# Sums of squares, first gate weights and output weights moved: three stages of an encoder-block kernel on one core

## The chip, the cores and the metric

The kernel runs on one core of one Trainium2 chip. The metric is the device time of one execution in microseconds (us), taken as the median of several runs.

The core's engines run side by side, each with its own queue of instructions: PE (TensorE) multiplies matrices into PSUM banks, PEld is its weight load, DVE (VectorE), ACT (ScalarE) and POOL (GpSimd) work element by element, and SP (SyncE) issues the loads and stores. An instruction that waits holds everything behind it on its own engine.

## The reference, cut to what matters

One encoder block on x of 1024 tokens by 1024 channels, all in float32:

```python
h = rmsnorm(x, norm_gain)
q, k, v, gate_a, u_in, v_in, gate_b, g_merge = split(h @ w_in)
q, k = rope(rmsnorm(q, q_gain)), rope(rmsnorm(k, k_gain))  # 8 q heads, 2 kv heads of 64
attn = block_attention(q, k, v) * silu(gate_a)
y_a = attn @ w_proj_attn
vv = layernorm(gelu(v_in))
v_mix = einsum('gij,bcjgd->bcigd', w_spatial, vv) + b_spatial
y_b = (gelu(u_in) * v_mix * silu(gate_b)) @ w_proj_gmlp
g = sigmoid(g_merge + b_merge)                             # two gates of 1024 channels
y = g[0] * y_a + g[1] * y_b
out = rmsnorm(x + y @ w_out, final_gain)
```

## The kernel before, in words

**Precision.** Each float32 operand is split into a rounded high part and a low part, the rest (`split`, line 115). The high part is a cast on the engine handed in (`hi_part`, line 107: lines 109 on POOL, 111 on ACT), the low part a subtraction, mostly on DVE (line 117). A product is then three matmuls: high by high, high by low, low by high (`mm3`, lines 175 to 177). So each block of weights or x costs one cast and one subtraction before PE can use it.

**Order.** The code is written stage after stage, and a scheduler then reorders the instructions of each engine within their dependences. Which buffer a tile gets is set by its tag and the number of buffers of that tag: a tile waits until the last reader of the buffer's former holder is done. PSUM has a tag "S" with three double banks, and single banks "o" and "z".

**Start.** `load_x` (line 146) brings the eight 128x1024 blocks of x transposed, multiplies them by the gain and splits them (line 159 on ACT, 160 on DVE). Each block goes straight into the k and v product (`kv`). High parts of the kv weights and the v weights are cast on POOL (`stream_w`, `nat_weights`, with `NWE` as the engines). Beside that, `add_square` squares every block on ACT (line 171, tiles of tag "og"); POOL and DVE add the squares up (line 172, `XSQ` names the engine of each block), and 16 small matmuls sum over the partitions (line 236, `ssx`). From them comes `rstd`, one over the root mean square of each token, and its half `rstdh`. `nat_group` makes the groups v0 to v3 in "S" banks; ACT moves each out with `rstdh` as the scale (line 371, `vst`). Then come GELU and layer norm of v (`v_post`), mixing over the 128 tokens of a chunk (`spatial`), the q groups, the norm of q and k (`head_norm`, line 319 for its last product) and the rotary positions (`rope`): their cross products stand on POOL (line 330, four of 128x256 for each q group and four for k). The tables behind them (line 395) and two scalings of v (lines 407 and 428) are POOL's too.

**Attention.** For each of 32 pairs PE makes two score tiles, softmax runs over DVE and ACT (lines 557 to 568), a DMA transposes the probabilities, and PE mixes them with v into the bank "o" (line 579, evacuated by lines 580 to 586). The products u, gate a and gate b fill PE between.

**Projections and gates.** `proj_b` makes the spatial branch's projection in eight blocks `yb0` to `yb7` (ACT copies each out, line 641), while `x_chunk` builds sums and differences of x (`xf`) for the gates. The gates and the other projection are done in pairs by `seven` products instead of eight. For each gate pair i, `pair_weights` (step "w" in the list `MORDER`) loads two rows of 512 KB (`graw`), squares their four quarters on ACT into the bank "o" (line 817, `gsq`), of which only the sums are kept, and makes a common scale from the sums (`unit_scale`, lines 673 to 680: a small matmul, DVE, POOL, DVE). `pair` (step "g") splits the scaled weights into two 16-bit parts (line 684 on ACT, 685 on DVE: `wg`) and multiplies. `p1g` is the copy of a pair's first product, to which the others are added (line 700). Step "A" makes the forms of the attention output (`gf`, `gk`), steps "a" project them (`wp`, `y`). Step "o" loads the output weights.

**Output weights and output product.** `out_weights` loads 16 halves of 256 KB through the four small `wraw` tiles, casts each (ACT, line 111, `woh`) and subtracts (DVE, line 117, `wol`). `split_y` splits the merged y blocks (lines 864 and 865). 384 matmuls make the output, and `finish` adds x (`xr`, line 950), takes the norm and stores.

## Time and profile before

| | before |
|---|---|
| runs | 766.96, 770.64, 770.91 us |
| median | 770.64 us |
| profiled execution | 771.03 us, of which the span is 769.3 us |
| PE busy | 94% of the span |
| VectorE, ScalarE, GpSimd busy | 80%, 57%, 21% |
| granted clock of TensorE, mean | 0.979 |

The span runs from the first to the last instruction on the chip; the time has some 1.7 us more around it. A row of the timeline gives start, length, engine, line, operation, the tiles it writes and reads, and in brackets how long its engine was idle before it and what ended that. A row of the grouped lines gives the count, busy time, the mean of one in ns and the idle time before them. In a row of windows each engine has its busy us and its number of instructions.

### The profile page before, as it was taken

To read this page: it belongs to the slowest core of one execution; us is meant where nothing else is said; L and a number is where in the kernel's file an instruction comes from. 1 tells how busy PE (TensorE), PEld (TensorE's weight loads), DVE (VectorE), ACT (ScalarE), POOL (GpSimd) and SP (SyncE) were. 2 spreads that over 40 slices of the span, in tenths; PEclk is the share of its full clock that TensorE was granted. 3 is DMA by queue.
4 is the path that set the end of the run, shared out by engine and by line. 5 is a ranking of instruction groups with operands and counts; after the bars stand their busy time and mean duration, and the time that the engine had idled before them with its cause. 6 is when DMAs were issued, how large, how long until landed. Compare 5 with 4: busy or idle time off the path is not lost.

```text
span 769.3 us, 9864 instructions
## 1 busy us (share of the span) xinstructions
PE 725.2 (94%) x3577; PEld 535.9 (70%) x3577; DVE 612.9 (80%) x915; ACT 434.7 (57%) x752; POOL 160.1 (21%) x131
## 2 busy tenths in 40 slices
PE   7989999998999899999999997899999998799996
PEld 7868888776888677788777884355464645388884
DVE  6965897699888989988889999999888898833223
ACT  7304457386878877878777478555474535521101
POOL 4930665345123221123200000010000000000000
PEclk9979999998999999999999999999999999999998
DMA  7321120135668779869899930130030204520211
GB/s 279 106 82 35 29 82 16 40 58 109 135 137 149 145 146 163 176 133 172 165 192 267 250 84 1 55 120 19 20 117 1 71 27 152 170 102 29 82 55 55
DMA packets 152609, 81.27 MB, mean 106 GB/s; under 512 B 135408, under 2 KB 136048, under 8 KB 152560
## 3 DMA queue, kind: packets, MB, share of 16 engines
q1 hardware_dynamic: 152272, 80.36, 42.5%
q8 instruction: 28, 0.46, 0.2%
q10 hardware_dynamic: 288, 0.28, 0.1%
q14 instruction: 21, 0.17, 0.1%
HBM read 42.88 MB, written 4.19 MB: 61 GB/s over the span
## 4 chain that ended last, share of the span: by engine, by line
PE 53%; DVE 21%; DMA 11%; ACT 6%; issue 6%; POOL 2%; SPq 1%; POOLq 0%; DVEq 0%; ACTq 0%
DMA T<-p 8%; PE out L175 4%; PE out L177 4%; PE out L176 4%; PE o L579 3%; DVE p L568 3%; DVE nm L557 2%; PE g L175 2%; PE g L176 2%; PE g L177 2%; DMA wraw<-in_wall_dram 2%; PE v L176 1%; PE v L177 1%; PE s L554 1%; PE v L175 1%
## 5 line engine op out<-in xcount | busy, mean ns | idle before, releaser
L568 DVE SCALAR_TENSOR_TENSOR p<-P,ri,p 128x1024 f16<-128x1024 f32 x64 | 85.8, 1343 | 22.2 <-ACT p L567 21.8
L567 ACT ACTIVATE p<-P,ri 128x1024 f16<-128x1024 f32 x64 | 73.1, 1143 | 25.1 <-DMA T<-p 17.4
L561 ACT ACTIVATE P<-s,nm 128x1024 f32<-128x1024 f32 x64 | 71.3, 1114 | 24.1 <-DVE nm L557 15.6
L557 DVE TENSOR_REDUCE nm<-s 128x1 f32<-128x1024 f32 x64 | 77.7, 1215 | 1.8 <-PE s L555 1.4
L579 PE MATMUL o<-T,vS 128*128 128x256 f16 x512 | 63.5, 278 | 4.9 <-ACT qT L355 2.9
L579 PEld LDWEIGHTS <-vS 128*128 128x128 f16 x512 | 48.2, 99 | 19.8 <-issue 8.0
L117 POOL TENSOR_TENSOR wl<-wraw,wh 128x512 fp32r<-128x512 f32 x24 | 38.8, 1620 | 101.3 <-ACT wh L111 57.4
L554 PE MATMUL s<-kT,qT 128*128 128x512 f32 x128 | 53.5, 418 | 4.0 <-ACT P L561 4.0
L677 POOL TENSOR_TENSOR scg<-scg,mhalf 128x1 f32<-128x1 f32 x8 | 7.0, 870 | 217.2 <-DVE scg L676 217.2
L555 PE MATMUL s<-kT,qT 128*128 128x512 f32 x128 | 50.5, 395 | 0.0
L950 DVE TENSOR_TENSOR xr<-out,xr 128x1024 f32<-128x1024 f32 x7 | 8.6, 1224 | 46.4 <-PE out L177 46.2
L898 ACT ACTIVATE sq<-xr 128x1024 f32<-128x1024 f32 x7 | 7.4, 1060 | 64.1 <-DVE xr L950 64.1
L175 PE MATMUL out<-woh,yhl 128*128 128x512 f32 x96 | 38.0, 396 | 0.0
L177 PE MATMUL out<-woh,yhl 128*128 128x512 f32 x96 | 37.6, 392 | 0.0
L176 PE MATMUL out<-wol,yhl 128*128 128x512 f32 x96 | 37.6, 391 | 0.0
L554 PEld LDWEIGHTS s<-kT,qT 128*128 128x128 f32 x128 | 24.1, 188 | 11.0 <-ACT P L561 6.4
L900 POOL TENSOR_TENSOR rs<-rs,mhalf 128x1 f32<-128x1 f32 x7 | 3.8, 549 | 125.5 <-DVE rs L899 125.5
L555 PEld LDWEIGHTS s<-kT,qT 128*128 128x128 f32 x128 | 24.1, 189 | 4.6 <-issue 0.2
L492 PE MATMUL ga<-xh,wh 128*128 128x512 f32 x64 | 26.1, 408 | 1.2 <-DVE ga30w L498 1.1
L175 PE MATMUL v<-nh,xh 128*128 128x512 f32 x64 | 26.8, 419 | 0.0
L492 PE MATMUL u<-xh,wh 128*128 128x512 f32 x64 | 25.6, 400 | 0.8 <-DVE uw L515 0.8
L177 PE MATMUL v<-nh,xl 128*128 128x512 f32 x64 | 26.1, 408 | 0.0
(554 smaller groups left out, 2212.9 us busy)
## 6 DMA issues: line engine op xcount, KB each, us to landing
wraw<-in_wall_dram SPq DMA_DIRECT2D x75, 256.0 KB, 3.1
graw<-in_wall_dram SPq DMA_DIRECT2D x16, 512.0 KB, 5.1
xraw<-in_xT_dram SPq DMA_DIRECT2D x15, 512.0 KB, 6.8
xr<-in_x_dram SPq DMA_DIRECT2D x8, 512.0 KB, 4.3
out_dram<-xr SPq DMA_DIRECT2D x7, 512.0 KB, 2.6
T<-p SPq DMA_TRANSPOSE x64, 4.5
wspr<-in_wsp_dram SPq DMA_DIRECT2D x2, 256.0 KB, 2.6
rtk<-in_cst_dram SPq DMA_DIRECT2D x1, 512.0 KB, 4.4
```

What stands on the lines that cost most here:

```text
L117: eng_lo.tensor_tensor(out=lo, in0=raw, in1=hi if hi.dtype == F16 else hi.bitcast(F32), op=ALU.subtract)
L175: pe.matmul(o, ah, bh, start=start, stop=False)
L176: pe.matmul(o, ah, bl, start=False, stop=False)
L177: pe.matmul(o, al, bh, start=False, stop=stop)
L492: pe.matmul(o, wh[:, C(dt % 4)], xh[dt][:, H(h)], start=(dt == 0), stop=False)
L554: pe.matmul(sp[:, H(hf)], qs, kT[:, 2 * v, H(hf)], start=True, stop=False)
L555: pe.matmul(sp[:, H(hf)], qs, kT[:, 2 * v + 1, H(hf)], start=False, stop=True)
L557: dve.tensor_reduce(out=nm, in_=sp, axis=AX.X, op=ALU.max, negate=True)
L561: act.activation(Pt, sp, AF.Exp, bias=nm, accum_out=rsum)
L567: act.activation(hi, Pt, AF.Copy, scale=ri)
L568: dve.scalar_tensor_tensor(out=lo, in0=Pt, scalar=ri, in1=hi, op0=ALU.mult, op1=ALU.subtract)
L579: pe.matmul(ot[:, 0:256], vS[:, kt, v, :], T[:, :, 8 * p + kt, :], start=(kt == 0 and p == 0), stop=(kt == 7 and p == 1))
```

## The change

Three stages are changed.

At the start, `add_square` now loads x a second time in its natural layout, eight blocks of 512 KB into the two "og" tiles, and squares each in place on ACT with the sum over the row as a second output (`ssx`). That gives the sum for each token without additions and without matmuls. It is called once behind each v weight (`between`). The high parts of kv, v and q weights and of the mixing weights go from POOL to ACT. The rotary cross products, the tables and both scalings of v go from POOL to DVE.

At the first gate, step "w0" (load, squares, scale of pair 0) leaves `MORDER` and is called in the loop of the spatial projection, behind its block 3.

At the output weights, whole rows of 512 KB are loaded into the eight "xh" tiles (`load_out`), and each row is split in one cast and one subtraction (`out_weight`) into other tiles. Two rows are split ahead of the last gate pair, the other six before the output product, and the tiles for x at the end (`xr`) change.

```diff
--- before
+++ after
@@ -46,8 +46,7 @@
     NWARM = 10
-    XSQ = (dve, dve, pool, pool, pool, pool, pool, dve)
-    NWE = (pool, pool)
+    NWE = (act, act)
     NWL = (dve, dve)
@@ -138,8 +137,6 @@
-    xsq = t4("rB", "xsq")
@@ -163,13 +160,13 @@
-    def add_square(dt, raw):
-        if dt == 0:
-            act.activation(xsq, raw, AF.Square)
-        else:
-            sq = t4("og", f"xsq{dt}")
-            act.activation(sq, raw, AF.Square)
-            XSQ[dt].tensor_tensor(out=xsq, in0=xsq, in1=sq, op=ALU.add)
+    ssx = const([P, NT], "ssx")
+    def add_square(tt):
+        xn = t4("og", f"xn{tt}")
+        nc.sync.dma_start(out=xn, in_=x[C(tt), :])
+        act.activation(xn, xn, AF.Square, accum_out=ssx[:, tt:tt + 1])
@@ -188,15 +185,14 @@
                 r = slice(256 * j, 256 * j + 256)
-                split(wh[:, r], wl[:, r], wr[:, r], pool)
+                split(wh[:, r], wl[:, r], wr[:, r], act)
             elif j == 0:
-                wh, wl = stream_w(W_KV + i // 2, i % 2)
+                wh, wl = stream_w(W_KV + i // 2, i % 2, act)
             r = slice(256 * j, 256 * j + 256)
...
                     dt == 0 and tt % 2 == 0, dt == 7 and tt % 2 == 1)
-            add_square(dt, raw)
@@ -207,7 +203,7 @@
-    def nat_weights(first, dts):
+    def nat_weights(first, dts, between=None):
         ws = []
@@ -218,6 +214,8 @@
             ws.append((hi[:, H(dt % 2)], l))
+            if between is not None:
+                between(dt)
         return ws
@@ -228,12 +226,10 @@
-    wv = nat_weights(W_VIN, range(8))
+    wv = nat_weights(W_VIN, range(8), add_square)
     ssp = ps_z("ssx")
-    for tt in range(NT):
-        pe.matmul(ssp[:, 2 * tt:2 * tt + 2], xsq[:, C(tt)], ones[:, 0:2], start=True, stop=True)
     gsq = small("gsq")
@@ -244,7 +240,7 @@
     rstd = const([P, NT], "rstd")
-    power_rstd(rstd, ssp[:, 0:16].rearrange("p (t k) -> p t k", k=2)[:, :, 0], NT, 1.0 / D)
+    power_rstd(rstd, ssx, NT, 1.0 / D)
     bmh = const([P, 16], "bmh")
@@ -260,7 +256,7 @@
         nc.sync.dma_start(out=raw, in_=wsp[:, H(h)])
-        split(wsh[:, H(h)], wsl[:, H(h)], raw, pool)
+        split(wsh[:, H(h)], wsl[:, H(h)], raw, act)
     bsp = t2("bsp")
@@ -327,7 +323,7 @@
             for b in range(2):
-                pool.tensor_tensor(out=t5[:, :, :, b, :], in0=s5[:, :, :, 1 - b, :],
+                dve.tensor_tensor(out=t5[:, :, :, b, :], in0=s5[:, :, :, 1 - b, :],
                                    in1=b5[:, :, :, b, :].broadcast_to([P, 8, 2, 16]), op=ALU.mult)
@@ -392,7 +388,7 @@
         for half in range(2):
-            pool.tensor_tensor(
+            dve.tensor_tensor(
                 out=heads(tab[half]), in0=heads(rtk[:, 0, H(half)]),
@@ -404,7 +400,7 @@
     v3 = vn.rearrange("p (t e) -> p t e", e=128)
-    pool.tensor_tensor(out=v3, in0=v3, in1=rstd[:, :, None].broadcast_to([P, 8, 128]), op=ALU.mult)
+    dve.tensor_tensor(out=v3, in0=v3, in1=rstd[:, :, None].broadcast_to([P, 8, 128]), op=ALU.mult)
     vscr = t2("vscr")
@@ -425,7 +421,7 @@
     dve.tensor_scalar(out=vsc, in0=vsc, scalar1=1.0 / (PSCALE * VSCALE), scalar2=None, op0=ALU.mult)
-    pool.tensor_tensor(out=v3, in0=v3, in1=vinv[:, None, :].broadcast_to([P, 8, 128]), op=ALU.mult)
+    dve.tensor_tensor(out=v3, in0=v3, in1=vinv[:, None, :].broadcast_to([P, 8, 128]), op=ALU.mult)
     v4 = vn.rearrange("p (t h d) -> p t h d", h=2, d=64)
@@ -736,7 +732,8 @@
     XCS = (0, 1, 3, 5)
-    MORDER = "w0 g0 w1 g1 w2 A a0 g2 w3 g3 w4 a1 g4 w5 g5 w6 a2 g6 w7 a3 o g7"
+    EARLY = 2
+    MORDER = "g0 w1 g1 w2 A a0 g2 w3 g3 w4 a1 g4 w5 g5 w6 a2 g6 w7 a3 o g7"
@@ -779,16 +776,6 @@
-    for j in range(2):
-        load_chunk(j)
-    for dt in range(8):
-        proj_b(dt)
-        if dt in XCS:
-            j = XCS.index(dt)
-            x_chunk(j)
-            if j + 2 < 4:
-                load_chunk(j + 2)
@@ -840,16 +827,41 @@
     gates, GA, pws, yas = {}, {}, {}, {}
+    for j in range(2):
+        load_chunk(j)
+    for dt in range(8):
+        proj_b(dt)
+        if dt in XCS:
+            j = XCS.index(dt)
+            x_chunk(j)
+            if j + 2 < 4:
+                load_chunk(j + 2)
+        if dt == 3:
+            pws[0] = pair_weights(0)
...
-    def out_weights():
-        lo4 = sb.tile([P, 4, 1024], F32R, tag="kT", bufs=1, name="wol")
+    wor, who4 = [], []
+    def load_out():
         for dt in range(8):
-            hi = t4("xh", f"woh{dt}", F32R)
-            lo = lo4[:, dt, :] if dt < 4 else t4("xl", f"wol{dt}", F32R)
-            for h in range(2):
-                split(hi[:, H(h)], lo[:, H(h)], load_w(W_OUT + dt, h), act, dve)
-            who.append((hi, lo))
+            raw = t4("xh", f"wor{dt}")
+            nc.sync.dma_start(out=raw, in_=wall[W_OUT + dt])
+            wor.append(raw)
+    def out_weight(dt):
+        if dt == 0:
+            who4.append(sb.tile([P, 4, 1024], F32R, tag="kT", bufs=1, name="who"))
+        if dt < 2:
+            hi, lo = who4[0][:, 2 * dt, :], who4[0][:, 2 * dt + 1, :]
+        else:
+            hi, lo = (t4(t, f"wo{dt}{k}", F32R) for k, t in enumerate(WOT[dt - 2].split()))
+        act.copy(hi, wor[dt])
+        dve.tensor_tensor(out=lo, in0=wor[dt], in1=hi.bitcast(F32), op=ALU.subtract)
+        who.append((hi, lo))
+    WOT = ("xl xl", "xh xh", "xh xh", "og og", "xh xh", "xh vS")
@@ -876,8 +888,9 @@
         elif step == "o":
-            out_weights()
-            for dt in range(2):
+            load_out()
+            for dt in range(EARLY):
+                out_weight(dt)
                 split_y(dt)
@@ -920,11 +933,13 @@
-    for dt in range(2, 8):
+    for dt in range(EARLY, 8):
+        out_weight(dt)
         split_y(dt)
-    xr = []
-    for i, tag in enumerate("og og vS rB P P p16 p16".split()):
-        xr.append(t4(tag, f"xr{i}"))
+    xr = [t4(tag, f"xr{i}") for i, tag in enumerate("P P p16 p16 rB".split())]
+    xr4 = sb.tile([P, 4, 1024], F32, tag="vm", bufs=1, name="xr4")
+    xr += [xr4[:, i, :] for i in range(3)]
+    for i in range(8):
         nc.sync.dma_start(out=xr[i], in_=x[C(i), :])
...
     nc.sync.dma_start(out=fg, in_=fgr)
```

The start on ScalarE's queue, before: `xh1` to `xh7` are the high parts of x, the rows of line 171 the squares of the same blocks.

```order
L159 ACTIVATE xh4_242<-xraw4_241,cs_65 128x1024
L171 ACTIVATE xsq4_277<-xraw4_241 128x1024
L159 ACTIVATE xh5_281<-xraw5_280,cs_65 128x1024
L171 ACTIVATE xsq5_310<-xraw5_280 128x1024
L159 ACTIVATE xh6_314<-xraw6_313,cs_65 128x1024
L171 ACTIVATE xsq6_349<-xraw6_313 128x1024
L159 ACTIVATE xh7_353<-xraw7_352,cs_65 128x1024
```

The same queue after the change: `nh` are high parts of the v weights, `xn` the blocks of x that are loaded for the squares.

```order
L156 ACTIVATE xh4_232<-xraw4_231,cs_65 128x1024
L110 CAST nh00_375<-wraw00_373 128x512
L169 ACTIVATE xn0_379,ssx_86<-xn0_379 128x1024
L169 ACTIVATE xn1_386,ssx_86<-xn1_386 128x1024
L156 ACTIVATE xh5_268<-xraw5_267,cs_65 128x1024
L156 ACTIVATE xh6_298<-xraw6_297,cs_65 128x1024
L110 CAST nh00_375<-wraw01_382 128x512
L156 ACTIVATE xh7_334<-xraw7_333,cs_65 128x1024
L110 CAST nh02_391<-wraw10_389 128x512
L110 CAST nh02_391<-wraw11_397 128x512
L110 CAST nh04_406<-wraw20_404 128x512
L169 ACTIVATE xn2_394,ssx_86<-xn2_394 128x1024
```

The squares no longer follow their block; they stand in pairs between the weight casts, the first pair ahead of `xh5`.

The first gate on ScalarE's queue, before: `gsq03` is the last square of pair 0, `gsq10` to `gsq13` are those of pair 1, `y47<-yb7` is the copy of the last block of the projection, and `wg011` the first weight of gate 0.

```order
L817 ACTIVATE gsq03_4594,gss0_4587<-graw0_4584 128x512
L817 ACTIVATE gsq10_4739,gss1_4738<-graw1_4735 128x512
L111 CAST xfT40_4274<-xraw1_4216 128x512
L111 CAST gf220_4920<-gat2_3895 128x1024
L817 ACTIVATE gsq11_4741,gss1_4738<-graw1_4735 128x512
L641 COPY y47_4207<-yb7_4552 128x1024
L111 CAST gk_4930<-gat2_3895 128x1024
L111 CAST xfT40_4274<-xraw4_4214 128x512
L817 ACTIVATE gsq12_4743,gss1_4738<-graw1_4735 128x512
L684 ACTIVATE wg011_4612<-graw0_4584,scg0_4598 128x512
```

And after:

```order
L804 ACTIVATE gsq03_4435,gss0_4428<-graw0_4425 128x512
L110 CAST xfT20_4262<-xraw4_4208 128x512
L110 CAST xfT40_4268<-xraw1_4210 128x512
L637 COPY y47_4201<-yb7_4571 128x1024
L110 CAST gk_4924<-gat2_3889 128x1024
L804 ACTIVATE gsq10_4733,gss1_4732<-graw1_4729 128x512
L110 CAST gf220_4914<-gat2_3889 128x1024
L804 ACTIVATE gsq11_4735,gss1_4732<-graw1_4729 128x512
L110 CAST xfT40_4268<-xraw4_4208 128x512
L804 ACTIVATE gsq12_4737,gss1_4732<-graw1_4729 128x512
L804 ACTIVATE gsq13_4739,gss1_4732<-graw1_4729 128x512
L680 ACTIVATE wg011_4606<-graw0_4425,scg0_4439 128x512
```

The squares of pair 0 still end just ahead of the last copies; all four squares of pair 1 and the form `gf220` now stand between the last copy and the first gate weight.

The loads of the output stage on SP's queue, before (`wraw490` to `wraw531` are halves of output weight rows, `xr` and `fg` what the end needs):

```order
L121 DMA wraw490_6101<-in_wall_dram 128x512
L121 DMA wraw491_6105<-in_wall_dram 128x512
L121 DMA wraw500_6111<-in_wall_dram 128x512
L121 DMA wraw501_6115<-in_wall_dram 128x512
L121 DMA wraw510_6121<-in_wall_dram 128x512
```

And after (`wor` are the whole rows):

```order
L850 DMA wor0_6066<-in_wall_dram 128x1024
L850 DMA wor1_6068<-in_wall_dram 128x1024
L850 DMA wor2_6070<-in_wall_dram 128x1024
L850 DMA wor3_6072<-in_wall_dram 128x1024
L850 DMA wor4_6074<-in_wall_dram 128x1024
L850 DMA wor5_6076<-in_wall_dram 128x1024
L943 DMA xr0_6266<-in_x_dram 128x1024
```

Sixteen half loads have become eight whole ones, six of them in a row ahead of the loads of x.

## Prediction

> **What bounds the kernel now.** I read the page first: whether one engine is full, and where it is not.
>
> ```profile
> span 769.3 us, 9864 instructions
> PE 725.2 (94%) x3577; PEld 535.9 (70%) x3577; DVE 612.9 (80%) x915; ACT 434.7 (57%) x752; POOL 160.1 (21%) x131
> ```
>
> TensorE is busy for 94% of the span, so a gain has to come from its pauses or from its clock. The windows view by stage shows where both are. Its columns are PE, weight loads, DVE, ACT and POOL busy, then granted clock, DMA share and GB/s.
>
> ```profile
> 28.00:44.00 16.00, 11.88 (x80) 10.29 (x79) 16.00 (x14) 2.52 (x5) 13.30 (x10) 0.98 0.30 97
> 44.00:60.00 16.00, 16.00 (x59) 13.04 (x58) 6.81 (x18) 0.75 (x2) 4.55 (x4) 0.70 0.15 50
> 81.40:156.00 74.60, 73.57 (x385) 61.92 (x384) 61.34 (x93) 40.09 (x66) 38.28 (x33) 1.00 0.14 43
> 156.00:200.00 44.00, 39.80 (x198) 31.18 (x197) 42.26 (x55) 32.62 (x65) 22.55 (x16) 0.92 0.48 94
> 634.00:673.00 39.00, 31.95 (x131) 16.23 (x130) 33.24 (x49) 22.11 (x35) 0.00 (x0) 0.96 0.49 158
> ```
>
> PE has four weak places: the start (VectorE and GpSimd full, ScalarE idle), the ramp into attention, the first gate (its rows are below) and the way into the output product. From 81.4 to 156 PE itself is the bound, so what is won before that should arrive at the ramp. A mean clock of 0.70 over 16 us, between full and half, is 9.6 us at half speed.
>
> The timeline of PE and ACT shows the start.
>
> ```profile
> 15.28 0.63 PE L175 MATMUL kv<-wh,xh 128*128 128x256 f32 x2
> 24.24 0.28 PE L175 MATMUL kv<-wh,xh 128*128 128x256 f32 x1
> 26.87 0.28 PE L176 MATMUL kv<-wl,xh 128*128 128x256 f32 x1
> 37.33 0.40 PE L175 MATMUL v<-nh,xh 128*128 128x512 f32 x1
> 41.85 1.13 PE L269 MATMUL wsum<-wspr,ones 128*128 128x512 f32 x2 [3.67 <-DMA wspr<-in_wsp_dram]
> 44.09 3.40 PE L236 MATMUL ssx<-ones,xsq 128*128 128x2 f32 x16
> 54.64 0.39 PE L175 MATMUL v<-nh,xh 128*128 128x512 f32 x1
> 58.06 0.39 PE L175 MATMUL v<-nh,xh 128*128 128x512 f32 x1
> 59.62 1.26 ACT L371 ACTIVATE vst<-v,rstdh 128x512 f32<-128x512 f32 x2 [15.05 <-PE v L177]
> ```
>
> The third kv block starts at 15.3, and the last product ahead of a pause of 3.7 us at 37.3; PE goes on at 41.9, at half clock, spends 3.4 us on sums of squares, and finishes the first v group only at 59.6. Two steps give the pitches: 2.63 us for 22 matmuls of 256 columns (0.12 each), 3.42 us for 15 of 512 (0.228).
>
> **The start, part by part.** Why VectorE is late, by the grouped lines of 13 to 42 us, beside the same subtractions with GpSimd idle (10.28 us) and over 176 to 460 us:
>
> ```profile
> L160 DVE SCALAR_TENSOR_TENSOR xl<-xraw,cs,xh 128x1024 fp32r<-128x1024 f32 x6 | 13.2, 2222 | 0.0
> L117 DVE TENSOR_TENSOR nl<-wraw,nh 128x512 fp32r<-128x512 f32 x7 | 10.6, 1544 | 0.0
> L172 DVE TENSOR_TENSOR xsq<-xsq,xsq 128x1024 f32<-128x1024 f32 x2 | 3.3, 1628 | 0.0
> 10.28 1.28 DVE L160 SCALAR_TENSOR_TENSOR xl<-xraw,cs,xh 128x1024 fp32r<-128x1024 f32 x1 [2.15 <-ACT xh L159]
> L117 DVE TENSOR_TENSOR wl<-wraw,wh 128x512 fp32r<-128x512 f32 x8 | 5.5, 682 | 0.0
> L172 POOL TENSOR_TENSOR xsq<-xsq,xsq 128x1024 f32<-128x1024 f32 x5 | 15.0, 3009 | 1.2 <-ACT xsq L171 1.2
> ```
>
> Beside a busy GpSimd a 512-column subtraction takes 1.54 us instead of 0.68, a 1024-column one 2.22 instead of 1.28. The change empties GpSimd here: no square sums, no high parts. VectorE then sheds 6 x 0.94, 7 x 0.86 and the 3.3 of its own square sums, 15 of 29 us. Per kv block PE needs 24 x 0.12 = 2.9 us, VectorE 1.28 + half of 0.68, so PE leads. ScalarE takes the high parts and squares:
>
> ```profile
> L111 ACT CAST wh<-wraw 128x512 fp32r<-128x512 f32 x3 | 1.9, 618 | 0.1
> xraw<-in_xT_dram SPq DMA_DIRECT2D x15, 512.0 KB, 6.8
> ```
>
> The squares change place, not number; some 13 casts of 0.62 add 8 us to an engine idle for 13.5 of the 16 us from 28 to 44. The new waits stand in ScalarE's queue: two squares wait for their x block with xh5 queued behind, later pairs hold back weight casts, and on SP each later pair waits for two squares to free its tiles, with weight loads behind. A block lands 6.8 us after its issue. The first pair, issued near 9, holds xh5 until about 19; PE wants xh5 at 15.3 + 3 x 2.9 = 24. Four rounds of 6.8 plus 2.4 end by 47, and the v scale a few us later. PE fills three PSUM tiles before it needs the scale, and the first mixing product, after v group 2, needs it only near 57. So this is covered by some 5 us at either end.
>
> Sum: 15.3 + 6 x 24 x 0.12 (17.3) + 48 x 0.228 (10.9) + a column sum (0.6) = 44.1 for the end of v group 0, against 59.6. I take **-14.5**, keeping 1 us for starts I can't see. It can be as little as -8, if VectorE keeps half its stretch, or -17.
>
> Rule against row: PE's 3.7 us pause is followed by 9.6 us at half clock, a loss of 4.8. The Trainium skill (TensorE: Matmul & The Clock Gate, Part 1: The HAM clock gate) says that one busy window of some 3.4 us opens the gate again, an estimated loss of 1.7; by that, 3.1 less would be won and the total would be 757.6. The measurement decides; the row shows longer.
>
> **81 to 156 and the ramp.** Moved onto VectorE are the rope products, the tables and two v scalings. GpSimd's rows, and VectorE's for like shapes:
>
> ```profile
> L330 POOL TENSOR_TENSOR qtmp<-qst,tabq 128x256 f32<-128x256 f32 x16 | 13.3, 859 | 7.8 <-DVE qst L319 7.8
> 460.31 0.41 DVE L117 TENSOR_TENSOR wp<-wraw,wp 128x256 fp32r<-128x256 f32 x1
> L117 DVE TENSOR_TENSOR nl<-wraw,nh 128x512 fp32r<-128x512 f32 x8 | 8.6, 1082 | 0.0
> ```
>
> Until 156 that is 12 x 0.41 + 4 x 0.68 and one v scaling, 1.28 by the xl row, = 8.9 us. VectorE is idle for 13.3 of those 74.6, and the eight weight subtractions alone give back 8 x 0.4 when the casts go to ScalarE. PE covers it: **0**, up to +8.9 without that cover. In the ramp 8 x 0.41 = 3.3 us come to a VectorE busy 42.3 of 44, less what its rows and waits beside GpSimd gave: **+1.5**, at most +3.3. At best PE's holes there close, 4.2 us idle and half of the 7 us at half clock: -7.7.
>
> A rule against it: the Trainium skill (SBUF — State Buffer, SBUF: two separate sides) locks one port pair for a whole instruction between GpSimd and VectorE operations with two SBUF inputs, as ropes have. GpSimd stays busy for about 16 of 44 us in the ramp, so eight ropes would meet it three times, 0.8 each: an estimate of 2.3 more and 756.8 in all. The stretched rows agree in kind.
>
> **First gate.** What stands before its first product:
>
> ```profile
> 462.46 0.57 DVE L586 TENSOR_TENSOR og<-o,o 64x128 f32<-64x128 f32 x2
> 464.09 0.61 ACT L817 ACTIVATE gsq<-graw 128x512 f32<-128x512 f32 x1
> 464.85 0.60 ACT L817 ACTIVATE gsq<-graw 128x512 f32<-128x512 f32 x1
> 470.20 0.99 ACT L641 COPY y<-yb 128x1024 f32<-128x1024 f32 x1
> 471.09 1.04 ACT L111 CAST gk<-gat 128x1024 fp32r<-128x1024 f32 x1
> 473.19 1.32 ACT L684 ACTIVATE wg<-graw,scg 128x512 f16<-128x512 f32 x2
> 473.95 0.61 PE L175 MATMUL g<-xf,wg 128*128 128x512 f16 x1 [5.41 <-ACT wg L684]
> ```
>
> The squares write into the bank that the last mix vacates at 463.0, so they can't move up by more than 1.1 us wherever the code puts them; the order confirms it, with the scale's product still behind all of the eighth block. But four squares of the second pair and a cast now stand behind the last block's copy: 4 squares at a pitch of 0.76 and two casts of 1.0 and one of 0.5, 5.5 us. PE has finished that block 5.41 us before 473.95, at 468.5, so the copy can end at 469.5, and the first weight comes at about 475.0, not 473.2. Some is regained, since the second pair is then done: **+1.5**, from -1.1 to +3.6 (another half-clock window).
>
> **Way into the output product.** ScalarE's casts stand in line behind small loads, VectorE behind the casts, PE behind both:
>
> ```profile
> 634.73 0.58 PE L175 MATMUL y<-gf,wp 128*128 128x512 f32 x1
> 651.25 1.29 ACT L111 CAST woh<-wraw 128x512 fp32r<-128x512 f32 x2 [4.67 <-DMA wraw<-in_wall_dram]
> 655.29 0.58 ACT L704 COPY p1g<-g 128x512 f32<-128x512 f32 x1
> 663.75 0.38 PE L175 MATMUL g7T<-xf,wg7T 128*128 128x512 f16 x1 [3.46 <-DVE ga L700]
> 673.01 0.58 PE L175 MATMUL out<-woh,yhl 128*128 128x512 f32 x1
> graw<-in_wall_dram SPq DMA_DIRECT2D x16, 512.0 KB, 5.1
> ```
>
> Now whole 512 KB rows go straight into the eight tiles that the attention forms leave. The first is free after six matmuls (636.1) and lands by 641.2; the fourth and fifth, which ScalarE casts ahead of p1g, are free near 644.5 to 645.5 and land by 650.5. Two casts later p1g runs at about 651.9 instead of 655.3: 3.4 us, and the loss behind the 3.46 hold (0.04 of 39 us of clock, 1.6) goes too: **-5**. If a load takes 6.8, +0.5; if all pauses go, the 38.3 from 634.7 to 673.0 less 132 products of 0.228 = -8.2. Later splits have 18 x 0.228 = 4.1 us of output product each as cover.
>
> **Sum.** -14.5 + 0 + 1.5 + 1.5 - 5 = -16.5, against the profiled 771.03 (span 769.3 plus 1.7 around it; 0.4 above the median of the runs): **754.5 us**.
>
> **Rivals.** *Given back:* from 81 on the chain of waits runs mostly through VectorE, and the added 8.9 and 3.3 lie on it: 754.5 + 8.9 + 1.8 = 765. For it: VectorE's near-full ramp; against: PE's 73.6 of 74.6. *Holes close too:* ramp -7.7 and out -8.2 instead of +1.5 and -5: 742. For it: the new order puts gate products before the first mix. Against: softmax keeps VectorE as full. *Slower:* VectorE's long rows aren't GpSimd's doing. Then only its square sums (3.3) and PE's (3.4) go at the start, while moved work runs at the long rate (1082/682 = 1.59): -6.7 + 14 + 5.2 + 1.5 - 5 = +9, 780. It decides if 512-column subtractions before 40 us stay above 1.2 us. The 0.68 rows speak against it.
>
> **Numbers.** Forecast 0.66 (749 to 760), given back 0.16, holes close 0.12, slower 0.06. 743 to 766 holds the forecast and half of the neighbours. A measurement can tell 0.5%, 3.9 us, from no change. Faster by more: 0.66 + 0.12 and most of the second, 0.88; same 0.06; slower 0.06.
>
> **What would show it.** Right: 0.7 us subtractions and no PE pause before 44 us, v group 0 out by 46, scores starting 14 us earlier, the gate's hold no shorter, out starting 5 us sooner than the shift. Wrong: PE waiting on casts queued behind squares, or a ramp longer by 5 us or more.

## The result, and the profile after

The changed kernel takes 747.49 us (median of 4 runs, 743.15 to 747.97) against 769.93 us for the kernel before in the same comparison. The ratio is 0.970, with a 95% interval of 0.966 to 0.975: faster by 3.0%. The forecast was 754.5 us, with a range of 743 to 766; its likeliest stretch, 749 to 760, was missed by 1.5 us. The profiled execution took 747.8 us, 23.2 less than the 771.03 of the one before.

The head of the page of the changed kernel:

```profile
span 746.0 us, 9814 instructions
PE 713.9 (96%) x3561; PEld 531.6 (71%) x3561; DVE 596.8 (80%) x931; ACT 446.2 (60%) x775; POOL 96.5 (13%) x77
```

PE is now busy for 96% of a span that is 23.3 us shorter; GpSimd has lost 64 us of work. The windows view, with the columns of the prediction (PE, weight loads, DVE, ACT, POOL, granted clock, DMA share, GB/s):

```profile
13.00:28.00 15.00, 15.00 (x113) 14.74 (x113) 11.49 (x14) 12.12 (x17) 0.00 (x0) 0.92 0.97 377
28.00:44.00 16.00, 16.00 (x97) 14.02 (x96) 5.15 (x12) 8.80 (x20) 0.00 (x0) 1.00 0.68 215
44.00:60.00 16.00, 16.00 (x70) 12.87 (x69) 11.76 (x26) 8.46 (x15) 3.19 (x3) 1.00 0.18 48
156.00:200.00 44.00, 36.58 (x192) 29.05 (x192) 37.06 (x53) 30.10 (x60) 10.87 (x6) 0.92 0.66 117
631.00:649.60 18.60, 18.59 (x87) 8.43 (x87) 17.77 (x23) 11.11 (x13) 0.00 (x0) 1.00 0.42 166
```

From 13 to 60 us PE does not pause any more (a pause of 2.13 us at 10.8, for `xh`, is left, where there was one of 1.73), and from 28 to 60 us it has the full clock. VectorE, full before, is busy for 5.15 of 16 us from 28 to 44. The last row is the stretch ahead of the output product: PE is full there too. The weak place that is left, and larger than before, is the ramp at 156 to 200: between the first and the 49th score product PE idles for 7.4 us, and did for 4.2 before. VectorE's grouped lines for 13 to 42 us, where the same blocks had 2222, 1544 and 1551 ns before:

```profile
L157 DVE SCALAR_TENSOR_TENSOR xl<-xraw,cs,xh 128x1024 fp32r<-128x1024 f32 x6 | 7.7, 1284 | 2.6 <-ACT xh L156 2.4
L116 DVE TENSOR_TENSOR nl<-wraw,nh 128x512 fp32r<-128x512 f32 x8 | 5.3, 687 | 2.2 <-ACT nh L110 2.0
L116 DVE TENSOR_TENSOR wl<-wraw,wh 128x512 fp32r<-128x512 f32 x3 | 2.1, 687 | 0.9 <-ACT wh L110 0.9
```

Two of PE's remaining pauses, in the ramp and at the first gate (a row has its start, its length, and in brackets the idle time before it):

```profile
159.46 0.80 PE L488 MATMUL ga<-xh,wh 128*128 128x512 f32 x1 [3.41 <-DVE uw L511]
457.53 0.59 PE L669 MATMUL usg<-gss,mhalf 128*128 128x4 f32 x2 [6.57 <-ACT gsq L804]
```

The following table cuts the profiled execution of each kernel at the starts of six products on PE, read from the timeline, in us: the last product of the v groups, the first score product, the 49th, the last of the spatial projection (yb), the first attention projection (y) and the first output product. All stages of a row are those of one kernel, so that a stage can be compared whatever the stages ahead of it did, as long as it holds the same work. At the 49th score it does not always: the stage before it holds 300 products in the kernels before, squares only and rotary products on GpSimd, 358 with the high parts and 324 with the ramp's rotary products on GpSimd, and 296 in all others. The experiments' rows are used below.

| kernel | v ends at | to first score | to 49th score | to end of yb | to first y | to output |
|---|---|---|---|---|---|---|
| before | 94.86 | 58.63 | 62.84 | 251.70 | 46.38 | 158.60 |
| changed | 81.52 | 56.90 | 65.93 | 245.83 | 48.46 | 150.98 |
| squares only | 80.91 | 57.30 | 63.64 | 247.86 | 46.54 | 158.22 |
| first stage only | 79.74 | 56.90 | 65.70 | 245.46 | 48.71 | 159.46 |
| high parts on GpSimd | 79.22 | 58.43 | 74.02 | 249.42 | 42.18 | 150.99 |
| rotary products on GpSimd | 80.59 | 58.68 | 64.71 | 246.75 | 50.45 | 151.01 |
| ramp's rotary products there | 79.48 | 56.92 | 65.95 | 255.68 | 44.14 | 151.00 |
| gate step back | 81.22 | 56.90 | 64.59 | 245.65 | 48.72 | 150.98 |
| squares into bank z | 79.08 | 56.92 | 64.64 | 245.77 | 48.43 | 150.98 |
| old output weights | 80.79 | 56.93 | 65.73 | 245.41 | 48.47 | 157.95 |
| GpSimd kept busy | 90.44 | 56.90 | 65.94 | 245.42 | 48.48 | 150.98 |
| GpSimd only writing | 80.17 | 56.90 | 65.88 | 245.94 | 48.47 | 151.01 |
| bank z and step back | 81.20 | 56.90 | 64.41 | 245.80 | 49.19 | 150.97 |

One execution among the experiments, the profiled one of the first run with the rotary products on GpSimd, took 1855 us, with products on PE about twice as long (0.86 us in place of 0.41 for a score product), and is left out; that row is from a second run of the same kernel.

So the 23.4 us up to the output product are 13.3 at the start, 1.7 in the q groups, minus 3.1 in the ramp, 5.9 in the rest of attention, minus 2.1 at the first gate, and 7.6 ahead of the output product.

### The profile page after: what moved, and what is told of

Its sections match the earlier page's. It is cut to its first block, busy times and chain, and to the rows that moved or that the text cites. A ratio compares the mean times of both kernels' runs of the same rounds, so it can differ in the third digit from the quotient of the medians.

```text
span 746.0 us, 9814 instructions
## 1 busy us (share of the span) xinstructions
PE 713.9 (96%) x3561; PEld 531.6 (71%) x3561; DVE 596.8 (80%) x931; ACT 446.2 (60%) x775; POOL 96.5 (13%) x77
## 4 chain that ended last, share of the span: by engine, by line
PE 79%; DVE 10%; DMA 4%; ACT 3%; issue 2%; POOL 1%; SPq 0%; POOLq 0%; DVEq 0%; ACTq 0%
PE o L575 6%; PE out L174 4%; PE out L173 4%; PE out L172 4%; DMA T<-p 3%; PE s L550 3%; PE s L551 3%; PE g L172 3%; PE g L173 3%; PE g L174 3%; PE q L172 2%; PE q L174 2%; PE v L172 2%; PE v L173 2%; PE v L174 2%; PE q L173 2%
## 5 line engine op out<-in xcount | busy, mean ns | idle before, releaser
L564 DVE SCALAR_TENSOR_TENSOR p<-P,ri,p 128x1024 f16<-128x1024 f32 x64 | 88.9, 1393 | 15.0 <-ACT p L563 14.6
L557 ACT ACTIVATE P<-s,nm 128x1024 f32<-128x1024 f32 x64 | 71.4, 1115 | 23.3 <-DVE nm L553 12.2
L575 PE MATMUL o<-T,vS 128*128 128x256 f16 x512 | 61.8, 273 | 2.2 <-DMA T<-p 2.2
L116 POOL TENSOR_TENSOR wl<-wraw,wh 128x512 fp32r<-128x512 f32 x24 | 36.2, 1508 | 112.2 <-ACT wh L110 96.8
L673 POOL TENSOR_TENSOR scg<-scg,mhalf 128x1 f32<-128x1 f32 x8 | 9.8, 1220 | 221.6 <-DVE scg L672 221.6
L110 ACT CAST wh<-wraw 128x512 fp32r<-128x512 f32 x35 | 21.5, 614 | 18.9 <-PE yb L173 7.5
L489 PE MATMUL ga<-xl,wh 128*128 128x512 f32 x64 | 26.2, 409 | 0.0
L490 PE MATMUL ga<-xh,wl 128*128 128x512 f32 x64 | 26.0, 407 | 0.0
L680 ACT ACTIVATE wg<-graw,scg 128x512 f16<-128x512 f32 x16 | 11.5, 721 | 24.1 <-PE g L174 12.8
L172 PE MATMUL yb<-gmh,wh 128*128 128x512 f32 x64 | 25.3, 397 | 0.4 <-ACT gmh L110 0.4
```

The lines of the kernel that those rows point to most:

```text
L116: eng_lo.tensor_tensor(out=lo, in0=raw, in1=hi if hi.dtype == F16 else hi.bitcast(F32), op=ALU.subtract)
L172: pe.matmul(o, ah, bh, start=start, stop=False)
L557: act.activation(Pt, sp, AF.Exp, bias=nm, accum_out=rsum)
L564: dve.scalar_tensor_tensor(out=lo, in0=Pt, scalar=ri, in1=hi, op0=ALU.mult, op1=ALU.subtract)
L575: pe.matmul(ot[:, 0:256], vS[:, kt, v, :], T[:, :, 8 * p + kt, :], start=(kt == 0 and p == 0), stop=(kt == 7 and p == 1))
```

## The experiments

My theory: the start is faster because GpSimd's additions no longer stretch VectorE's rows, the output stage because whole rows land earlier, and the gate step's new place does nothing. Rivals: the casts or the rotary products are what counted; the long rows had another cause; the gate step's move matters.

**Is it GpSimd that stretches VectorE's rows?** Two runs add work to GpSimd at the start of the changed kernel, on a tile that nothing reads. On all other engines the instructions and their order stay the same, but for one row of VectorE in the second run.

```diff
+    dm = t4("rB", "dm")
+    pool.memset(dm, 0.0)
+    for i in range(12):
+        pool.tensor_tensor(out=dm, in0=dm, in1=dm, op=ALU.mult)
     kvs = [ps_s(f"kv{b}") for b in range(2)]
```

> The changed kernel with 12 multiplications of 128x1024 on GpSimd added at the start, on a tile of its own that nothing reads; every other engine has the same instructions in the same order. If a busy GpSimd stretches VectorE's rows of two SBUF inputs, the 512-column subtractions while it runs go from 0.69 to 1.2 us or more and the first v group comes out 4 to 12 us later: 751 to 759. If the long rows before had another cause (load, order, the loads of x), they stay at 0.7 and the time at 747.5 within 1 us.

It took 755.95 us (754.97 to 756.58; ratio to before 0.984, 0.982 to 0.986), 8.5 above the changed kernel. VectorE's and GpSimd's grouped lines for 8 to 42 us, and PE's longest pause:

```profile
L157 DVE SCALAR_TENSOR_TENSOR xl<-xraw,cs,xh 128x1024 fp32r<-128x1024 f32 x7 | 16.9, 2442 | 0.0
L116 DVE TENSOR_TENSOR wl<-wraw,wh 128x512 fp32r<-128x512 f32 x3 | 7.1, 2378 | 0.0
L116 DVE TENSOR_TENSOR nl<-wraw,nh 128x512 fp32r<-128x512 f32 x6 | 5.6, 964 | 0.2 <-ACT nh L110 0.2
L179 POOL TENSOR_TENSOR dm<-dm 128x1024 f32<-128x1024 f32 x10 | 24.7, 2469 | 0.7
```

```profile
28.97 0.58 PE L174 MATMUL kv<-wh,xl 128*128 128x256 f32 x1 [3.78 <-DVE xl L157]
```

Beside the multiplications a row of 1024 columns takes 2.44 us on average instead of 1.28 (the last of the seven stands behind them), one of 512 takes 2.38 instead of 0.69, and PE starves on the same line as before the change. The v groups end 9 us later, and no other stage in the table moves by more than 0.5. The `nl` rows, most of them behind the last multiplication, are near their old rate. The second run puts fills in place of the multiplications:

```diff
+    for i in range(20):
+        pool.memset(dm, 0.0)
```

> As the run before, but the added work on GpSimd only writes: 20 fills of 128x1024 of the same tile, no input. If the contention needs an operation of GpSimd that reads SBUF, VectorE's subtractions stay at 0.7 us and the time at 747.5 within 1 us. If any use of SBUF by GpSimd does it, they are stretched as in the run before, to 1.0 us or more while it runs, and the time is 749 or more.

It took 746.22 us (745.82 to 746.86; ratio 0.972, 0.969 to 0.974). VectorE and GpSimd, 8 to 42 us:

```profile
L157 DVE SCALAR_TENSOR_TENSOR xl<-xraw,cs,xh 128x1024 fp32r<-128x1024 f32 x7 | 9.0, 1285 | 6.7 <-ACT xh L156 6.5
L116 DVE TENSOR_TENSOR wl<-wraw,wh 128x512 fp32r<-128x512 f32 x3 | 2.0, 687 | 0.0
L178 POOL MEMSET dm<- 128x1024 f32 x14 | 13.4, 955 | 0.7
```

Fills that only write cost VectorE nothing here. A busy GpSimd is not enough; the operations that stretched VectorE's rows also read SBUF. The Trainium skill (SBUF — State Buffer, SBUF: two separate sides) says the same of VectorE operations with two SBUF inputs, and both runs agree with it: 2442 against 1285 ns.

**Is it the additions alone?** The kernel before, with only the squares changed; casts, rotary products, gate and output weights stay.

```diff
-    wv = nat_weights(W_VIN, range(8))
+    wv = nat_weights(W_VIN, range(8), add_square)
-            add_square(dt, raw)
-    for tt in range(NT):
-        pe.matmul(ssp[:, 2 * tt:2 * tt + 2], xsq[:, C(tt)], ones[:, 0:2], start=True, stop=True)
```

(cut; `add_square`, `nat_weights` and `rstd` as in the change)

> The kernel before with one thing changed: the squares come from x loaded again and summed by ScalarE, with no additions on GpSimd or VectorE and no small matmuls. High parts, rotary products, tables and scalings stay on GpSimd, gate and output weights as before. If GpSimd's additions of two SBUF inputs were what stretched VectorE's rows, the last product of the v groups moves from 94.9 us to between 79 and 82, VectorE's 512-column subtractions before 42 us fall to 1.0 us or less, and the time is 752 to 757. If casts on GpSimd and moved rotary products were an essential part of the start's gain, that product stays above 86 us and the time above 760.

It took 754.34 us (753.12 to 755.96; ratio 0.980, 0.976 to 0.984). VectorE and GpSimd, 8 to 42 us:

```profile
L158 DVE SCALAR_TENSOR_TENSOR xl<-xraw,cs,xh 128x1024 fp32r<-128x1024 f32 x7 | 10.2, 1462 | 4.0 <-ACT xh L157 4.0
L116 DVE TENSOR_TENSOR nl<-wraw,nh 128x512 fp32r<-128x512 f32 x8 | 6.5, 826 | 0.5 <-POOL nh L108 0.5
L116 DVE TENSOR_TENSOR wl<-wraw,wh 128x512 fp32r<-128x512 f32 x3 | 2.8, 955 | 0.0
L108 POOL TENSOR_SCALAR nh<-wraw 128x512 fp32r<-128x512 f32 x8 | 7.8, 979 | 10.0 <-DMA wraw<-in_wall_dram 10.0
```

The v groups end at 80.9, as in the changed kernel. So the squares bring all 13 to 14 us of the start. The eleven casts on GpSimd stretch the subtractions only to 0.83 and 0.96, and VectorE has room for that: it waits 4.0 us for `xh`. The edit takes away GpSimd's additions together with VectorE's own (3.3 us) and PE's 16 small products (3.4 us); no run separates the three.

**The high parts back on GpSimd**, in the changed kernel:

```diff
-    NWE = (act, act)
+    NWE = (pool, pool)
-                split(wh[:, r], wl[:, r], wr[:, r], act)
+                split(wh[:, r], wl[:, r], wr[:, r], pool)
```

(and the same in `stream_w`'s call and for the mixing weights)

> The changed kernel with the high parts of the kv, v, q and mixing weights back on GpSimd; the squares stay on ScalarE with their own loads. If a busy GpSimd stretches VectorE's rows (the prediction's reason), the 512-column subtractions before 42 us are well above 0.69 us (1.0 to 1.5), and the first v group comes out 2 to 6 us later: 750 to 754. If the gain came from the square sums that left VectorE and GpSimd alone, or from the 16 small matmuls that left PE, the subtractions stay below 0.8 us and the time within 1.5 us of 747.5.

It took 754.28 us (752.19 to 756.19; ratio 0.981, 0.976 to 0.986). The time is where the theory put it, but the reason is not: the v groups end at 79.2, no later, with subtractions of 0.82 and 0.96 us. The 10.9 us that it has more up to the end of yb are 1.5 in the q groups, 8.1 up to the 49th score and 3.6 after it, less 2.3 at the start. The 8.1 are mostly moved work, with 62 more products ahead of the 49th score: PE's pauses there are shorter than in the changed kernel, 4.9 against 7.4 us. Behind it they are 11.7 against 2.4 us, with 13.7 us at half clock where the changed kernel has none. Behind the end of yb the first gate and its neighbours give 6.3 back. PE's pauses at the end of attention in this kernel, from four places of the timeline:

```profile
389.02 0.51 PE L550 MATMUL s<-kT,qT 128*128 128x512 f32 x1 [2.44 <-ACT P L557]
...
397.20 0.80 PE L550 MATMUL s<-kT,qT 128*128 128x512 f32 x1 [3.17 <-ACT P L557]
...
406.96 0.69 PE L172 MATMUL yb<-gmh,wh 128*128 128x512 f32 x1 [2.73 <-ACT P L557]
```

The scheduler has put scores, mixing and fillings into another order, with scores left at the end that wait for softmax and nothing to fill PE. Both my theory and the rival had looked only at the start.

**The rotary products back on GpSimd**, with the tables and the scalings of v, in the changed kernel:

```diff
-                dve.tensor_tensor(out=t5[:, :, :, b, :], in0=s5[:, :, :, 1 - b, :],
+                pool.tensor_tensor(out=t5[:, :, :, b, :], in0=s5[:, :, :, 1 - b, :],
```

(and the same for the tables and both scalings)

> The changed kernel (747.5 us) with the rotary cross products, the tables and both scalings of v back on GpSimd; all else as changed. The prediction's step: these moves cost nothing up to 156 us and +1.5 in the ramp, so undoing them gives 746, and at best 744. Rival: GpSimd's detour (products of 0.86 us that VectorE waits for, and VectorE's own rows stretched beside them) costs more than VectorE's extra rows, so undoing them is slower, 750 to 756, with VectorE's 512-column subtractions between 60 and 160 us back near 1.1 us instead of 0.69.

It took 749.19 us (748.22 to 750.45; ratio 0.975, 0.970 to 0.980). The kernel ran once more, for its stages; the text on record calls it the first experiment, and its 48th score product is the 49th of the table:

> The first experiment's kernel again, since its profiled execution ran at half speed throughout and its stages can't be read. From its other runs 748 to 751. If the smaller pauses of attention after 216 us (6 us won) come from the rotary products having left GpSimd, they are back here, while the ramp up to the 48th score product is 3 us shorter. If they come from the order that follows from the start, both stay as in the changed kernel within 1.5 us.

748.24 us (746.15 to 750.75; ratio 0.972, 0.967 to 0.976). VectorE's grouped lines of 60 to 160 us, first of this kernel, then of the changed one:

```profile
L116 DVE TENSOR_TENSOR nl<-wraw,nh 128x512 fp32r<-128x512 f32 x8 | 8.0, 1018 | 0.0
L116 DVE TENSOR_TENSOR vl<-vg,vh 128x512 fp32r<-128x512 f32 x6 | 5.7, 942 | 0.0
```

```profile
L116 DVE TENSOR_TENSOR nl<-wraw,nh 128x512 fp32r<-128x512 f32 x8 | 5.4, 690 | 0.7 <-ACT nh L110 0.5 <-issue 0.2
L116 DVE TENSOR_TENSOR vl<-vg,vh 128x512 fp32r<-128x512 f32 x6 | 4.0, 683 | 2.2 <-ACT vh L110 2.1
```

The subtractions are stretched again, as the rival said, and yet the time hardly moves, less than either side expected: the q groups take 1.8 us more, the ramp 1.2 less. The gain after the 49th score does not go with the rotary products: 246.8 us here, 245.8 in the changed kernel, 251.7 before. The difference of the two kernels, 0.7 to 1.7 us by the medians, lies within the uncertainty.

**Only the ramp's rotary products back on GpSimd** (those of the last two q groups):

```diff
-        rope(qst, tmp, Aq[:, 2 * g:2 * g + 2], Bq[:, 2 * g:2 * g + 2], 2, 8)
+        rope(qst, tmp, Aq[:, 2 * g:2 * g + 2], Bq[:, 2 * g:2 * g + 2], 2, 8, (dve, dve, pool, pool)[g])
```

(cut; the cross products in `rope` run on the engine handed in)

> The changed kernel with the rotary products of the last two q groups alone, those that fall into the ramp, back on GpSimd. If VectorE's queue is what opens PE's pause of 3.41 us near 159 us in the ramp, the ramp shrinks by 2 to 3 us and the time is 744.5 to 746. If GpSimd's detour costs as much there, or the order at the end of attention changes again, 747 to 751.

It took 752.43 us (751.33 to 753.78; ratio 0.978, 0.973 to 0.983), above both expected ranges. The stage up to the 49th score is as long as in the changed kernel (65.95 against 65.93), but it holds 28 more filling products, and PE's pauses in it are 2.6 us instead of 7.4. The pause of 3.41 us is shorter, and the end of attention is 9.9 us longer:

```profile
156.33 0.50 PE L488 MATMUL ga<-xh,wh 128*128 128x512 f32 x1 [2.31 <-DVE uw L511]
...
403.24 0.79 PE L172 MATMUL yb<-gmh,wh 128*128 128x512 f32 x1 [4.86 <-ACT P L557]
```

So an edit at the ramp's start goes with another order 200 us later. That is the second such case. In both, the way from the first score to the end of yb is about 10 us longer (323.4 and 321.6 us against 311.8), though but for two products PE does the same work in it.

**The gate step back at the head of the list**, in the changed kernel:

```diff
-        if dt == 3:
-            pws[0] = pair_weights(0)
-    MORDER = "g0 w1 g1 w2 A a0 g2 w3 g3 w4 a1 g4 w5 g5 w6 a2 g6 w7 a3 o g7"
+    MORDER = "w0 g0 w1 g1 w2 A a0 g2 w3 g3 w4 a1 g4 w5 g5 w6 a2 g6 w7 a3 o g7"
```

> The changed kernel with the first gate's step back at the head of the list of steps instead of behind block 3 of the spatial projection. The prediction says that the place in the code moves nothing, since the squares wait for the bank of the last mix: 747.5 within 1 us, with the first gate's pause at 6 to 7 us. Rival: the move itself is what makes PE's pause longer (6.57 us now, 5.41 before) or what makes it shorter than it would be: then the time moves by 1.2 us or more, and the pause with it.

It took 745.60 us (744.06 to 746.24; ratio 0.970, 0.965 to 0.974): the change's second stage brings nothing. The profiled execution is 1.6 us shorter than the changed kernel's, but not at the gate, where the stage takes 48.72 us against 48.46: 1.3 of it lie in the ramp, where TensorE is at half clock for 3.4 us instead of 6.8. PE's pauses at the gate are as long:

```profile
449.89 0.38 PE L669 MATMUL usg<-gss,mhalf 128*128 128x4 f32 x2 [1.13 <-ACT gsq L804]
...
455.94 0.59 PE L669 MATMUL usg<-gss,mhalf 128*128 128x4 f32 x2 [5.67 <-ACT gsq L804]
```

**The squares of the gate weights into another bank**, in the changed kernel:

```diff
     def junk(name):
-        return ps_o(name)
+        return ps_z(name)
```

> The changed kernel with one line changed: the squares of the gate weights are written into bank z, which the last filling product has left, instead of bank o, which the last mix holds. If that bank is what keeps the squares late, as the prediction said, they move up among the blocks of the projection, PE's pause of 6.57 us before the first gate shrinks below 2 us and the time is 741 to 743. If ScalarE's queue or the forms of x hold the first gate anyway, the pause keeps 4 us or more and the time 745 to 748.

It took 745.98 us (744.02 to 747.40; ratio 0.971, 0.968 to 0.974). The squares do move up: the first scale's product starts at 413.7 instead of 450.6, and the first gate's at 446.6 right behind the projection. But from there to the first y it takes 48.43 us, as before this edit. VectorE in the stretch behind it, and three of PE's new pauses:

```profile
446.00:470.00 24.00, 16.87 (x66) 6.60 (x65) 24.00 (x37) 12.19 (x17) 0.94 (x1) 0.86 0.00 1
```

```profile
453.99 0.38 PE L173 MATMUL g<-xfT,wg 128*128 128x512 f16 x1 [1.35 <-DVE xfT L116]
...
457.65 0.38 PE L172 MATMUL g0T<-xf,wg0T 128*128 128x512 f16 x1 [1.78 <-ACT p1g L700]
...
461.37 0.59 PE L172 MATMUL g0T<-xf,wg0T 128*128 128x512 f16 x1 [1.83 <-DVE ga L696]
```

VectorE is busy for 24.0 of 24.0 us with the forms of x and of the attention output. The one long pause has become several short ones, with the same sum of 8.6 us up to the first y. So the bank did hold the squares, but freeing it doesn't bring the 741 to 743 us that were expected with that. Both edits together:

> The changed kernel with both small gains at the first gate: squares into bank z and the gate step back at the head of the list of steps. If VectorE's forms hold the first gate once the squares are out of the way, as the run with bank z alone shows (VectorE busy for 24.0 of 24.0 us from 446 to 470), the two don't add: 745 to 746.5, with the same string of short pauses behind the first gate. If each gives its own 1.0 to 1.3 us, 743.5 to 744.5.

746.40 us (744.84 to 747.71; ratio 0.971, 0.968 to 0.974): they don't add up. No version tried is faster than the changed kernel by more than the uncertainty.

**The old output weights**, in the changed kernel:

```diff
-            load_out()
-            for dt in range(EARLY):
-                out_weight(dt)
+            out_weights()
+            for dt in range(2):
                 split_y(dt)
```

(cut; `out_weights` and the tiles for x as before)

> The changed kernel with the old output weights: halves of 256 KB through four small tiles, all split ahead of the last gate pair, x loaded into the old tiles. The prediction gave this stage 5 us, at most 8.2: 752.5 to 755.7, with pauses of PE of 3 us or more between the last projection and the output product. If the 7.6 us that the two traces show between the first projection of the attention branch and the output product come from the order in other stages, the time stays below 750.

It took 753.79 us (753.26 to 756.09; ratio 0.982, 0.976 to 0.987), 6.3 above the changed kernel. Behind the start, the only stage that differs by more than 0.5 us is the last: 157.95 instead of 150.98. PE's longest pause there is the one of before:

```profile
646.42 0.59 PE L172 MATMUL g7T<-xf,wg7T 128*128 128x512 f16 x1 [4.02 <-DVE ga L696]
```

**The first stage alone**: the changed kernel with the gate step and the output weights as before.

> Only the first stage of the change: the kernel before with its start changed (squares from x loaded again, high parts on ScalarE, rotary products, tables and v scalings on VectorE), the gate step and the output weights as before. By the prediction's terms 771 - 14.5 + 1.5 = 758 against 771.0 profiled, so about 757 as a median. If attention's smaller pauses (some 6 us won between 216 and 450 us, which the prediction did not have) come from the start's change too, 751 to 753; if they come from the later stages' buffers, 756 to 758.

It took 752.02 us (750.08 to 754.00; ratio 0.979, 0.976 to 0.982). The stages up to the first y are those of the changed kernel, attention's gain included (245.5 us after the 49th score).

## Why the prediction was right, point by point

**Start: -14.5 forecast, -13.3 measured at the end of the v groups.** The mechanism holds: additions of GpSimd stretched VectorE's rows, and without them PE is the bound. The kernels with the start changed and GpSimd left alone end the v groups between 79.1 and 81.5 us, so single executions differ by more than the 1.2 us that are missing. Much of that spread is one stretch of half clock near 12 us: executions with it (changed, gate step back, old output weights, bank z and step back) end at 80.8 to 81.5, executions without it (first stage only, ramp's rotary products, bank z) at 79.1 to 79.7; the kernel before has it too. PE's pause of 3.67 us before was ended by a load (`wspr`), but that is VectorE's lateness too: SP's queue stood for 15.6 us on VectorE's `nl` rows and issued that load at 39.1, and after the change at 28.2. PE starts the last of the first v group's 48 products at 44.9 instead of 59.2, where the sum had 44.1 and 1 us kept for starts. The price of the half clock behind the pause was rightly taken from the row: it lasted 10.2 us before and is gone, where one window of 3.4 us would have given 3.1 us less. The forecast that the group would be out by 46 us was a little early. ScalarE and VectorE around that point in the changed kernel:

```profile
47.68 0.69 ACT L367 ACTIVATE vst<-v,rstdh 128x512 f32<-128x512 f32 x1 [2.61 <-DVE rstdh L247]
```

```profile
45.10 0.17 DVE L131 TENSOR_SCALAR rstd<-ssx 128x8 f32<-128x8 f32 x1 [1.97 <-ACT xn L169]
47.42 0.17 DVE L247 TENSOR_SCALAR rstdh<-rstd 128x8 f32<-128x8 f32 x1 [0.94 <-POOL rstd L132]
```

The last square ends near 45 and the scale is ready at 47.6, where I had put both "by 47, and the v scale a few us later". PE was covered by its three PSUM tiles, as said. The part about which cast counts was wrong in weight: I listed square sums and casts together, and the casts could have stayed.

**81 to 156: 0 forecast, -1.7 measured** up to the first score. With the rotary products back on GpSimd this is 58.68 instead of 56.90, and VectorE's own rows are 1.02 instead of 0.69 us. But with squares only, where these products and the casts are on GpSimd too, it is 57.30, so most of the 1.7 us comes without their move.

**Ramp: +1.5 forecast, at most +3.3; +3.1 measured** up to the 49th score. The term was in its range but near the wrong end. PE's pause of 3.41 us is set by this string on VectorE in the changed kernel:

```profile
154.05 1.94 DVE L564 SCALAR_TENSOR_TENSOR p<-P,ri,p 128x1024 f16<-128x1024 f32 x1
155.92 1.21 DVE L330 TENSOR_TENSOR qst<-qst,qtmp 128x1024 f32<-128x1024 f32 x1
157.05 0.15 DVE L560 RECIPROCAL ri<-ri 128x1 f32<-128x1 f32 x1
157.12 1.68 DVE L277 SCALAR_TENSOR_TENSOR ut<-ut,uw 128x512 f32<-128x512 f32 x1
158.72 0.68 DVE L511 TENSOR_TENSOR uw<-u,rB 128x512 f32<-128x512 f32 x1
```

PE's next product needs the bank that the last row frees. The rows with 1.94 and 1.68 us run beside subtractions on GpSimd. With the ramp's rotary products back on GpSimd the pause is 2.31 us, and 1.19 (close behind another of 1.53) with all of them there, so VectorE's load does bear on it; the order changed in both runs too, and no run separates the two. For like work the term is past its bound: the stage has four products fewer than before, some 0.9 us at 0.228 each, which makes it +4.0, and the rest of attention -6.8. The rule that eight rotary products would meet GpSimd three times at 0.8 us each did not come out in size: seven of the eight took 0.40 to 0.41 us, and one, at 178.1 beside a subtraction on GpSimd, took 1.52.

**Rest of attention: nothing forecast, -5.9 measured.** This term was missing, and it is the largest error. With the ramp, attention from the first score to the end of yb is 2.8 us shorter, where +1.5 was forecast. PE's pauses behind the 49th score are 7.3 us before, 3.8 with squares only and 2.4 in the changed kernel. The longest two of before, and the one longer than 0.5 us that squares only has behind 260 us:

```profile
376.44 0.50 PE L554 MATMUL s<-kT,qT 128*128 128x512 f32 x1 [1.56 <-ACT P L561]
410.93 0.51 PE L492 MATMUL ga<-xh,wh 128*128 128x512 f32 x1 [1.06 <-DVE ga30w L498]
```

```profile
358.75 0.50 PE L551 MATMUL s<-kT,qT 128*128 128x512 f32 x1 [0.60 <-ACT P L558]
```

The gain comes with the first stage (245.5 us there) and for two thirds with the squares alone (247.9). It does not come from the rotary products. The two runs with the long tails suggest that the order alone can move attention by 10 us. But a new order is not needed for the two thirds: behind the 49th score, squares only has the order of before on VectorE (one row more at the very end) and on ScalarE, and on PE but for a few products that change places in the first 31 us. What shortens the pauses there stays open.

**First gate: +1.5 forecast, +2.1 measured.** That the new place moves nothing was right, and the run with the step back confirms it. I had put the longer wait down to it all the same. It comes with the first stage instead, since the kernel with that stage alone has it too (48.71), and not with the squares alone (46.54). Of the +2.1, PE's pauses are 1.0 (8.6 against 7.6 us), and TensorE is at half clock for 6.8 us instead of 3.4, the further stretch that the forecast had at its upper end. What ends the pause is also more than I said: in PE's queue the scale of pair 1 stands ahead of gate 0's first product, so PE waits for all eight squares.

**Way into the output product: -5 forecast, -7.6 measured**, near the -8.2 of all pauses closed. The mechanism is right, as 6.97 us in that stage come back with the old weights: PE's pauses in it are 7.0 us before and with the old weights, 2.2 in the changed kernel, and a stretch of 3.4 us at half clock is gone. The term was too small. I sized it by the copy `p1g` standing behind ScalarE's casts. ScalarE in the changed kernel:

```profile
632.79 1.05 ACT L860 CAST wo<-wor 128x1024 fp32r<-128x1024 f32 x1 [1.99 <-DVE wo L861]
634.47 0.59 ACT L700 COPY p1g<-g 128x512 f32<-128x512 f32 x1 [0.63 <-PE g L174]
```

The copy now waits for PE, not for a weight, so what I took for a shorter wait is none.

**Rivals.** *Given back* (765) and *slower* (780) did not happen: VectorE took the moved rotary rows at 0.44 us per 256 columns, and the long rows were GpSimd's doing. *Holes close too* (742) happened at the output, not in the ramp. The time lies nearer to that rival's 742 than to 754.5, but not by its mechanism.

**Right, with some luck.** The five terms forecast come to -17.4 us where -16.5 were forecast; that this is so close is in part luck, since their errors (+1.2, -1.7, +1.6, +0.6, -2.6) cancel. The -5.9 that no term forecast comes on top and takes the time below 749. Together they are the -6.8 us between forecast and measurement (6.7 by the profiled times).

## What to carry to other kernels

Before moving work onto an idle engine, look whether that engine's operations read SBUF beside VectorE's two-input rows: the same subtraction took 0.69 us alone, 0.83 to 0.96 beside casts, 1.54 beside casts and additions, and 2.4 on average beside multiplications that never stop. Undo a change stage by stage, cut the timelines at the same products, and count the products in each stage before comparing its length: here one of three stages did nothing, and of the first stage one edit brought nearly all. Where a scheduler orders the queues, an edit can move stages far behind it by several us; keep such a term in the range.

## What was not expected of the hardware

TensorE's half clock comes in steps of 3.41 us. By the granted clock in slices of 0.5 us, it lasted 3.4 us at the start of the changed kernel (12.0 to 15.4), 6.8 behind the pause of 3.41 us (158.7 to 165.6), 6.8 behind the 6.57 us (455.7 to 462.5), and 10.2 behind the 3.67 us of the kernel before (43.3 to 53.5). With bank z and pauses of at most 1.83 us it still fell, from 458.8 to 465.6.

Cutting the traces into windows of 3.41 us at these times tells more than the longest pause does. The clock fell behind windows in which PE was busy for 0.73 us (158.7), for none (455.7), for 1.45 (43.3) and, with bank z, for 1.32: several short pauses count together. It stayed at half behind a first window that held part of the pause or pauses, with PE busy for 2.69, 1.35 and 1.40 us (158.7, 455.7, bank z), and rose behind the second, with 3.41, 3.32 and 3.16. The stretch of 10.2 us does not fit: the profile has PE busy throughout all three of its windows, the first of them mostly with the 16 products of two columns. The Trainium skill (TensorE: Matmul & The Clock Gate, Part 1: The HAM clock gate) gives the window as 3413 ns and lets one busy window open the gate; the traces agree, but for that stretch.
